# Adding up the value pairs of layer A's x and x1 on GpSimd before the product, and taking two tiles step by step together

## The chip, the cores and the metric

The kernel runs on one core of one Trainium2 chip. The metric is the device time of one execution in microseconds (us), lower is better. Before the change it is 2796.8 us, the median of three runs (2795.46 to 2797.88).

A core has five engines that run their own instruction queues in order and wait for one another by semaphores: TensorE (PE: matrix products and transposes; its weight loads are shown as PEld), VectorE (DVE), ScalarE (ACT), GpSimd (POOL) and SyncE (SP), which here issues nearly all transfers.

## The reference, cut to what matters

Sequence length 2048, width 1024, one layer A and one layer B, all in float32. The change touches layer A after its pooling mixer: the output projection with its residual (giving x1), and the gated embedding (giving x2).

```python
def reference(x, p, ...):
    for i in range(DEPTH):                      # DEPTH = 2
        if i < N_A:                             # layer A, i = 0
            h = rms_norm(x, a_norm[i])
            x = x + pool_mixer(h, a_w_in[i], a_w_group[i], a_scale[i], a_w_out[i])   # x1
        else:                                   # layer B: attention against shared K/V
            ...
            x = x + (o * jax.nn.silu(z)) @ b_w_out[j]
        x = x + (p[i] @ ple_w[i]) * jax.nn.sigmoid(x @ ple_gate_w[i])                # x2 for i = 0
    return x
```

## The kernel before

All activations of layer A are kept transposed: 8 tiles of 128 channels by 512 positions (index o = 0..7). The 2048 positions are worked in four chunks, s = 0..3. To keep float32 accuracy in products whose operands TensorE takes in a rounded form, each operand is stored as a **pair**: a tile [128, 2, 512] whose first half is the value rounded by a ScalarE copy, and whose second half is the rest, value minus rounded value (`split`, lines 213 to 215). A product takes three matmuls for each pair of operands (`product`, lines 131 to 133): high weight by high activation, high by low, low by high. The sum of the two halves of a pair is the value itself, up to float32 rounding.

Per chunk there are 22 steps, in this order: 4 times two steps for the z and u halves of the input projection (groups g = 3, 2, 1, 0; `run_z`, `run_u`, the latter with the pooling), 4 steps of the output projection (`run_o`, b = 0..3), 4 steps of the gate (`run_g`, b = 0..3), and 6 steps for q, k and v (`run_kvq`). After the last chunk comes the attention (layer B). Each step of `run_o` and `run_g` makes two output tiles, o = 2b and 2b + 1, each with 8 x 3 matmuls over the 8 input tiles, the two tiles interleaved; `run_g` adds 12 matmuls with the embedding p. Weights are loaded and split one step ahead (line 718): from HBM into `wraw`, ScalarE copies the high half (L106, or L112 with a gain), GpSimd or VectorE subtracts for the low half (L108, or L113 on VectorE). In the same steps, some weights of layer B are split and stored for later (`keep`: kraw, kpair).

The code is given to a scheduler that orders the instructions of each engine ahead of time; where the order matters to the author it is pinned (`keep_in_program_order`). At run time each engine takes its list in that order.

Around the change:

- `run_o` multiplies the mixer's output (tiles mp) by the output weights into PSUM (psd). The first two steps put off the last two input tiles.
- `residual` makes x1: VectorE adds PSUM and the high half of x's pair (L467), GpSimd adds the low half (L468), then ScalarE's copy (L214) and VectorE's subtraction (L215) make x1's pair, one tile after the other.
- `load_p` transposes the embedding p (L482) and splits it (ple).
- `run_g` multiplies all 8 x1 pairs by the gate weights, in the order o = 0..7, and ple by its weights; then, tile by tile, sigmoid on ScalarE (L498), multiply on VectorE (L499), add x1's low half on GpSimd (L500), add its high half on VectorE (L502), store the sum (L503), split it into x2's pair (L214, L215), store that (L507), square it (L510) and add the squares over the tiles (L513).
- `run_kvq` multiplies the 8 x2 pairs, again in the order 0..7, by the q, k and v weights (L525). After its first 48 matmuls, L534 sums the squares over the channels.
- `tmp` gives tiles of one rotating pool of 8 buffers, shared by the tiles ta, sg, tx, sq, po, zr and others.

So TensorE comes to the tiles x1[6], x1[7] 36 and 42 matmuls into the first gate product of a chunk, and to x2[6], x2[7] 36 and 42 matmuls into the first q product; these tiles are made by the step just before.

Of the kernel before, what the change touches and what calls it, by code (L numbers as in the profile page):

```python
# [10 lines left out]
AF = mybir.ActivationFunctionType  # L11
ALU = mybir.AluOpType
# [17 lines left out]
def f(ap):  # L30
    return ap.bitcast(F32)
# [3 lines left out]
def trunk_kernel(ctx, tc, x, p, a_norm, a_w_in, a_w_group, a_scale, a_w_out, kv_norm, w_kv,  # L35
                 k_norm, b_norm, b_w_in, b_q_norm, b_w_out, ple_w, ple_gate_w, out):
    nc = tc.nc
    V, A, G, T = nc.vector, nc.scalar, nc.gpsimd, nc.tensor
# [81 lines left out]
    def wst(units, kt, hl, c0, n=P):  # L120
        kk = units[0].shape[2]
        return units[kt // kk][:, hl, kt % kk, c0 : c0 + n]

    def product(pss_, units, acts, c0s, order=None, beside=(), begin=True, end=True):


        beside = iter(beside)
        order = order or range(len(acts))
        for kt in order:
            for ps, c0 in zip(pss_, c0s):  # L130
                T.matmul(ps, wst(units, kt, 0, c0), acts[kt][:, 0], start=(begin and kt == order[0]), stop=False)  # L131
                T.matmul(ps, wst(units, kt, 0, c0), acts[kt][:, 1], start=False, stop=False)  # L132
                T.matmul(ps, wst(units, kt, 1, c0), acts[kt][:, 0], start=False,  # L133
                         stop=(end and kt == order[-1]))
            next(beside, None)
        for _ in beside:
            pass
# [6 lines left out]
    def pair(nm):  # L144
        return act.tile([P, 2, W5], F32R, tag="act", name=nm)
# [33 lines left out]
    with ExitStack() as st:  # L179
# [7 lines left out]
        def dense():  # L187
            state["d"] += 1
            return (psd if state["d"] % 3 else psboth).tile([P, W5], F32, tag="psd", name="psd")

        def turned():
            return pst.tile([P, 4, P], F32, tag="pst", name="pst")

        def tmp(nm):
            return t2.tile([P, W5], F32, tag="tmp", name=nm, bufs=8)
# [17 lines left out]
        def split(pr, src, lo):  # L213
            A.copy(out=pr[:, 0], in_=src)  # L214
            lo.tensor_tensor(out=pr[:, 1], in0=src, in1=f(pr[:, 0]), op=ALU.subtract)  # L215
# [198 lines left out]
        def run_u(s, g, wu):  # L414
# [4 lines left out]
            for k in range(2):  # L419
# [24 lines left out]
                else:  # L444
                    split(pr, po, V)

        def run_o(s, b, wo):
            ck = chunk[s]
            pss2 = [dense(), dense()]
            if b < 2:  # L450
                product(pss2, wo, ck["m"], (0, P), [6, 7, 4, 5, 2, 3], end=False)
                if not b:
                    ck["o"] = pss2, wo
                    return
                for (pss2, wo), b in ((ck.pop("o"), 0), ((pss2, wo), 1)):
                    product(pss2, wo, ck["m"], (0, P), [0, 1], begin=False)
                    residual(s, b, pss2)
                return
            product(pss2, wo, ck["m"], (0, P))
            residual(s, b, pss2)  # L460

        def residual(s, b, pss2):
            ck = chunk[s]
            for k in range(2):
                xp = ck["x"][2 * b + k]
                t = tmp("ta")
                V.tensor_tensor(out=t, in0=pss2[k], in1=f(xp[:, 0]), op=ALU.add)  # L467
                G.tensor_tensor(out=t, in0=t, in1=f(xp[:, 1]), op=ALU.add)  # L468
                pr = pair("x1")
                split(pr, t, V)  # L470
                ck.setdefault("x1", []).append(pr)

        def load_p(s):
            pin = [io.tile([P, 2, PLE], F32, tag="io", name="pin") for _ in range(2)]
            for e in range(2):
                t0 = s * W5 + e * 2 * P
                nc.sync.dma_start(out=pin[e], in_=p[0, 0, t0 : t0 + 2 * P, :].rearrange("(j q) n -> q j n", q=P))
            col = []
            for k in range(2):
                pt = turned()  # L480
                for j in range(4):
                    T.transpose(pt[:, j, :], pin[j // 2][:, j % 2, k * P : (k + 1) * P], ident)  # L482
                pr = pair("ple")
                split(pr, pt.rearrange("q j t -> q (j t)"), V)
                col.append(pr)
            chunk[s]["p"] = col

        def run_g(s, b, wg, wl):
            ck = chunk[s]
            if b == 0:  # L490
                load_p(s)
            pss2, pls = [dense(), dense()], [dense(), dense()]
            product(pss2, wg, ck["x1"], (0, P))
            product(pls, wl, ck["p"], (0, P))
            for k in range(2):
                o = 2 * b + k
                sg = tmp("sg2")
                A.activation(out=sg, in_=pss2[k], func=AF.Sigmoid)  # L498
                V.tensor_tensor(out=sg, in0=pls[k], in1=sg, op=ALU.mult)  # L499
                G.tensor_tensor(out=sg, in0=sg, in1=f(ck["x1"][o][:, 1]), op=ALU.add)  # L500
                t = tmp("tx2")
                V.tensor_tensor(out=t, in0=sg, in1=f(ck["x1"][o][:, 0]), op=ALU.add)  # L502
                nc.sync.dma_start(out=x2d[s][o], in_=t)  # L503
                pr = pair("x2")
                split(pr, t, V)
                if s + 1 < NSUB:
                    nc.sync.dma_start(out=x2p[s][o], in_=f(pr))  # L507
                ck.setdefault("x2", []).append(pr)
                sq = tmp("sq")
                A.activation(out=sq, in_=t, func=AF.Square)  # L510
                if o:
                    na = t2.tile([P, W5], F32, tag="acc", name="acc")
                    G.tensor_tensor(out=na, in0=ck["acc"], in1=sq, op=ALU.add)  # L513
                    sq = na
                ck["acc"] = sq
# [152 lines left out]
        for s in range(NSUB):  # L668
            for g in (3, 2, 1, 0):
                def load(g=g, s=s, z=0):  # L670
                    if not s and z and g < 3:
                        chunk[0]["fold"][g] = load_fold(g)
                    if not s and not z:
                        return (None,)
                    return (load_w(wp, a_w_in[0], KT, z * D + g * 256, 256, g_a, "wi"),)
                steps.append((lambda load=load: load(z=1), lambda *w, s=s, g=g: run_z(s, g, *w)))
                steps.append((load, lambda *w, s=s, g=g: run_u(s, g, *w)))
            for b in range(4):
                steps.append((lambda b=b: (load_w(wp, a_w_out[0], KT, b * 256, 256),),
                              lambda *w, s=s, b=b: run_o(s, b, *w)))  # L680
            for b in range(4):
                steps.append((lambda b=b: (load_w(wp, ple_gate_w[0], KT, b * 256, 256),
                                           load_w(wp, ple_w[0], 2, b * 256, 256)),
                              lambda *w, s=s, b=b: run_g(s, b, *w)))
            for kind, wsrc, base, gain in (("q", b_w_in[0], 0, g_b), ("k", w_kv, 0, g_kv), ("v", w_kv, D, g_kv)):
                for b in range(2):
                    def load(wsrc=wsrc, base=base, b=b, gain=gain, s=s, kind=kind):
                        return (load_w(wp, wsrc, KT, base + b * W5, W5, gain),)
                    steps.append((load, lambda *w, s=s, kind=kind, b=b: run_kvq(s, kind, b, *w)))
# [27 lines left out]
        for i, (_, run) in enumerate(steps):  # L717
# [10 lines left out]
            step, s = i % STEPS, i // STEPS  # L728
# [320 lines left out]
```

## Time and profile before

| | before |
|---|---|
| median of three runs | 2796.8 us (2795.46 to 2797.88) |
| profiled execution, its own time | 2798.39 us |
| its span, first to last instruction | 2796.3 us |
| mean granted TensorE clock | 0.996 |

The profile is of one execution. Its page gives the busy time of each engine; other views group instructions by line, list waits (who waited for whom, in total, how often, and the longest), or show instructions in order of time. In such a timeline a row has the start in us, the duration in us, engine, line and operation, the tile written and the tiles read, the shapes, how many instructions were merged into the row, and in brackets the idle time of the engine just before it and what ended it. The view by windows gives for a stretch of time its length and the busy time (and count) of PE, PEld, DVE, ACT and POOL, then the granted clock, the share of the transfer engines and GB/s; asked for one engine alone, it gives that engine's column only.

### The profile page before, as it was taken

How to read it: one execution, taken by the hardware profiler on the slowest of the kernel's cores; microseconds unless marked ns; L12 is line 12 of the kernel's file. 1: busy time of each engine (PE TensorE's matmuls, PEld its weight loads, DVE VectorE, ACT ScalarE, POOL GpSimd, SP SyncE). 2: the span in 40 equal slices, each digit the busy share in tenths (PEclk: the TensorE clock that was granted, in tenths of full speed). 3: DMA queues.
4: the chain of work that ended last, by engine and by line, in shares of the span. 5: the costliest groups of instructions: out<-in, count | busy, mean ns of one | idle time of the engine just before them, and what ended most of it. 6: DMA issues, size and time to landing. Idle time of an engine off the chain costs nothing. (4 is left out here: it accounts for less than half of the span.)

```text
span 2796.3 us, 40450 instructions
## 1 busy us (share of the span) xinstructions
PE 2739.2 (98%) x13715; PEld 2265.2 (81%) x13715; DVE 1892.1 (68%) x2573; ACT 1388.3 (50%) x2801; POOL 928.9 (33%) x949
## 2 busy tenths in 40 slices
PE   9999999999999999999999999999999999999999
PEld 7878888878887888878878888887878778878877
DVE  6645634455354543545499999999999988885642
ACT  5434533355234552345356566566666665564431
POOL 2554336543475424753222112112211122213220
PEclk9999999999999999999999999999999999999999
DMA  8654696546955489444678565555555565658865
GB/s 284 239 173 160 231 315 230 181 166 220 339 194 192 157 258 315 151 145 151 196 252 276 181 222 169 170 163 185 162 162 163 183 184 183 200 181 250 256 202 161
DMA packets 335844, 573.28 MB, mean 205 GB/s; under 512 B 32463, under 2 KB 166639, under 8 KB 335637
## 3 DMA queue, kind: packets, MB, share of 16 engines
q1 hardware_dynamic: 330186, 563.03, 61.9%
q10 hardware_dynamic: 5450, 7.66, 0.9%
q8 instruction: 108, 1.77, 0.3%
q14 instruction: 100, 0.81, 0.1%
HBM read 430.01 MB, written 132.19 MB: 201 GB/s over the span
## 5 line engine op out<-in xcount | busy, mean ns | idle before, releaser
L525 PE MATMUL psd<-wpair,x 128*128 128x512 f32 x2304 | 548.4, 394 | 4.5 <-ACT x L214 3.6
L802 ACT CAST at<-psa 128x512 fp32r<-128x512 f32 (+3 forms) x640 | 333.0, 521 | 396.0 <-PE psa L799 390.3
L785 DVE TENSOR_TENSOR_SCAN pp<-kap,pp,zeros 128x512 f32<-128x512 f32 x384 | 508.0, 1324 | 5.5 <-ACT kap L778 3.9
L525 PEld LDWEIGHTS psd<-wpair,x 128*128 128x128 f32 x2304 | 429.5, 189 | 93.5 <-ACT x L214 5.0
L803 DVE TENSOR_TENSOR at<-psa,at 128x512 fp32r<-128x512 f32 (+3 forms) x640 | 379.7, 595 | 57.6 <-ACT at L802 54.9
L799 PE MATMUL psa<-ident,pp 128*128 128x128 f32 x2176 | 346.5, 275 | 21.7 <-DVE at L803 17.6
L778 ACT ACTIVATE kap<-psl 128x512 f32<-128x512 f32 (+3 forms) x640 | 343.7, 538 | 18.4 <-PE psl L775 15.1
L799 PEld LDWEIGHTS psa<-ident,pp 128*128 128x128 f32 x2176 | 263.4, 140 | 99.7 <-DVE at L803 42.2
L774 PE MATMUL psl<-kk,qa 128*128 128x512 f32 (+3 forms) x640 | 280.6, 438 | 0.7 <-ACT kap L778 0.7
L780 POOL TENSOR_SCALAR_AFFINE_SELECT kap<-kap 128x128 f32<-128x128 f32 x256 | 92.2, 361 | 558.1 <-ACT kap L778 534.7
L785 DVE TENSOR_TENSOR_SCAN pp<-kap,zeros 128x128 f32<-128x128 f32 (+3 forms) x256 | 215.9, 844 | 43.0 <-POOL kap L780 38.4
L811 PE MATMUL pso<-at,vv 128*128 128x512 f32 (+3 forms) x640 | 234.6, 367 | 1.3 <-ACT at L802 1.2
L812 PE MATMUL pso<-at,vv 128*128 128x512 f32 (+3 forms) x640 | 235.5, 368 | 0.0
L775 PE MATMUL psl<-kk,qb 128*128 128x512 f32 (+3 forms) x640 | 234.1, 366 | 0.0
L131 PE MATMUL psd<-xp,wpair 128*128 128x512 f32 x512 | 202.2, 396 | 1.7 <-ACT xp L268 1.2
L132 PE MATMUL psd<-xp,wpair 128*128 128x512 f32 x512 | 200.6, 392 | 0.0
L133 PE MATMUL psd<-xp,wpair 128*128 128x512 f32 x512 | 200.3, 391 | 0.0
L113 DVE SCALAR_TENSOR_TENSOR wpair<-wraw,gains,wpair 128x512 fp32r<-128x512 f32 x192 | 151.8, 811 | 31.2 <-ACT wpair L112 30.9
L108 POOL TENSOR_TENSOR wpair<-wraw,wpair 128x512 fp32r<-128x512 f32 x99 | 137.9, 1402 | 87.0 <-ACT wpair L106 66.8
L112 ACT ACTIVATE wpair<-wraw,gains 128x512 fp32r<-128x512 f32 x192 | 134.0, 717 | 35.4 <-PE psd L525 33.8
L811 PEld LDWEIGHTS pso<-at,vv 128*128 128x128 f32 x640 | 120.5, 188 | 28.0 <-ACT at L802 2.3
L812 PEld LDWEIGHTS pso<-at,vv 128*128 128x128 f32 x640 | 120.4, 188 | 24.7
(210 smaller groups left out, 5399.9 us busy)
## 6 DMA issues: line engine op xcount, KB each, us to landing
kk<-kd SPq DMA_DIRECT2D x320, 128.0 KB
vv<-vd SPq DMA_DIRECT2D x160, 256.0 KB
wraw<-in_w_kv_dram SPq DMA_DIRECT2D x128, 256.0 KB
wpair<-wzd SPq DMA_DIRECT2D x64, 512.0 KB
wpair<-wod SPq DMA_DIRECT2D x64, 512.0 KB
wpair<-wgd SPq DMA_DIRECT2D x64, 512.0 KB
wpair<-wu SPq DMA_DIRECT2D x48, 512.0 KB
wpair<-wi SPq DMA_DIRECT2D x36, 512.0 KB
```

The lines of the kernel that those rows point to most:

```text
L131: T.matmul(ps, wst(units, kt, 0, c0), acts[kt][:, 0], start=(begin and kt == order[0]), stop=False)
L132: T.matmul(ps, wst(units, kt, 0, c0), acts[kt][:, 1], start=False, stop=False)
L525: T.matmul(pss2[i], ck["x2"][kt][:, xh, tk], wst(ws, kt, wh, 0, W5), start=(kt == 0 and xh == 0 and wh == 0), stop=(kt == KT - 1 and wh == 1))
L774: T.matmul(ps[:, :w], qa[:, qs], kk[:, :w], start=True, stop=False)
L775: T.matmul(ps[:, :w], qb[:, qs], kk[:, :w], start=False, stop=True)
L778: A.activation(out=kp[:, r0:], in_=ps[:, :w], func=AF.Sigmoid, scale=-1.0)
L785: V.tensor_tensor_scan(out=pp[:, r0:][:, ::-1], data0=kp[:, r0:][:, ::-1], data1=zeros.to_broadcast([P, w]), initial=1.0 if st["diag"] els ...
L799: T.transpose(pt[:, j * P : (j + 1) * P], pp[:, r0 + kt * P : r0 + (kt + 1) * P], ident)
L802: A.copy(out=at[:, 0, cs], in_=pt[:, cs])
L803: V.tensor_tensor(out=at[:, 1, cs], in0=pt[:, cs], in1=f(at[:, 0, cs]), op=ALU.subtract)
L811: T.matmul(po[:, cs], vv[:, kt, :], at[:, 0, cs], start=(st["diag"] and kt == 0), stop=False)
L812: T.matmul(po[:, cs], vv[:, kt, :], at[:, 1, cs], start=False, stop=(st["last"] and kt == 3))
```

## The change

A helper `whole` adds the two halves of pairs on GpSimd into new `tmp` tiles. `run_o` and `run_g` call it at their start, ahead of the product; `residual` and `run_g` then make one VectorE add each with the whole value, where before a VectorE add of the high half and a GpSimd add of the low half were made. In both places the two tiles of a step are also taken together: both sums, then both splits; in `run_g` both sigmoids, then multiply and add for each, then stores and splits, then squares.

```diff
+        def whole(prs, nm):
+            ts = []
+            for pr in prs:
+                ts.append(tmp(nm))
+                G.tensor_tensor(out=ts[-1], in0=f(pr[:, 0]), in1=f(pr[:, 1]), op=ALU.add)
+            return ts
+
         def run_o(s, b, wo):
             ck = chunk[s]
+            ts = whole(ck["x"][2 * b : 2 * b + 2], "ta")
             pss2 = [dense(), dense()]
             if b < 2:
                 product(pss2, wo, ck["m"], (0, P), [6, 7, 4, 5, 2, 3], end=False)
                 if not b:
-                    ck["o"] = pss2, wo
+                    ck["o"] = pss2, wo, ts
                     return
-                for (pss2, wo), b in ((ck.pop("o"), 0), ((pss2, wo), 1)):
+                for (pss2, wo, ts), b in ((ck.pop("o"), 0), ((pss2, wo, ts), 1)):
                     product(pss2, wo, ck["m"], (0, P), [0, 1], begin=False)
-                    residual(s, b, pss2)
+                    residual(s, ts, pss2)
                 return
             product(pss2, wo, ck["m"], (0, P))
-            residual(s, b, pss2)
-
-        def residual(s, b, pss2):
+            residual(s, ts, pss2)
+
+        def residual(s, ts, pss2):
             ck = chunk[s]
-            for k in range(2):
-                xp = ck["x"][2 * b + k]
-                t = tmp("ta")
-                V.tensor_tensor(out=t, in0=pss2[k], in1=f(xp[:, 0]), op=ALU.add)
-                G.tensor_tensor(out=t, in0=t, in1=f(xp[:, 1]), op=ALU.add)
+            for t, ps in zip(ts, pss2):
+                V.tensor_tensor(out=t, in0=ps, in1=t, op=ALU.add)
+            for t in ts:
                 pr = pair("x1")
                 split(pr, t, V)
                 ck.setdefault("x1", []).append(pr)
...
             if b == 0:
                 load_p(s)
+            ts = whole(ck["x1"][2 * b : 2 * b + 2], "tx2")
             pss2, pls = [dense(), dense()], [dense(), dense()]
             product(pss2, wg, ck["x1"], (0, P))
             product(pls, wl, ck["p"], (0, P))
+            sgs = [tmp("sg2"), tmp("sg2")]
             for k in range(2):
-                o = 2 * b + k
-                sg = tmp("sg2")
-                A.activation(out=sg, in_=pss2[k], func=AF.Sigmoid)
-                V.tensor_tensor(out=sg, in0=pls[k], in1=sg, op=ALU.mult)
-                G.tensor_tensor(out=sg, in0=sg, in1=f(ck["x1"][o][:, 1]), op=ALU.add)
-                t = tmp("tx2")
-                V.tensor_tensor(out=t, in0=sg, in1=f(ck["x1"][o][:, 0]), op=ALU.add)
+                A.activation(out=sgs[k], in_=pss2[k], func=AF.Sigmoid)
+            for k in range(2):
+                V.tensor_tensor(out=sgs[k], in0=pls[k], in1=sgs[k], op=ALU.mult)
+                V.tensor_tensor(out=ts[k], in0=sgs[k], in1=ts[k], op=ALU.add)
+            for k in range(2):
+                o, t = 2 * b + k, ts[k]
                 nc.sync.dma_start(out=x2d[s][o], in_=t)
                 pr = pair("x2")
                 split(pr, t, V)
                 if s + 1 < NSUB:
                     nc.sync.dma_start(out=x2p[s][o], in_=f(pr))
                 ck.setdefault("x2", []).append(pr)
+            for k in range(2):
+                o, t = 2 * b + k, ts[k]
                 sq = tmp("sq")
                 A.activation(out=sq, in_=t, func=AF.Square)
```

In the changed code the add in `whole` is line 452, the add in `residual` line 474, the sigmoid 505, multiply and add 507 and 508.

## The prediction

> **What bounds the kernel now.** I read the page first, then TensorE's list of waits, then its timeline around those waits, then the granted clock there. The page has TensorE busy for all but 57.1 us of the span.
>
> ```profile
> PE 2739.2 (98%) x13715; PEld 2265.2 (81%) x13715; DVE 1892.1 (68%) x2573; ACT 1388.3 (50%) x2801; POOL 928.9 (33%) x949
> ```
>
> So a change to the other engines can only give back time in which TensorE stands still or runs slowly. Its list of waits holds four entries that the changed lines feed (columns: total us, times, longest):
>
> ```profile
> PE psd L131 <- ACT x L214: 4.7, 5, 3.3
> PE psd L525 <- ACT x L214: 3.6, 3, 2.2
> ...
> PE psd L132 <- DVE x L215: 1.6, 5, 0.6
> ...
> PE psd L525 <- DVE x L215: 0.9, 4, 0.2
> ```
>
> L131 and L132 wait for x1 (written by the residual of the output projection, read by the gate product), L525 waits for x2 (written by the gate step, read by the q product). Recorded idle time: 4.7 + 3.6 + 1.6 + 0.9 = 10.8 us. That is too small a price, because matmuls overlap and the record of one ends late. I therefore price each wait by start times. A clean spacing comes from 42 matmuls in 9.68 us (first row below): less the 0.39 of the last one, 9.29 / 41 = 0.227 us each, so 48 take 10.88.
>
> ```profile
> 180.32 0.48 PE L131 MATMUL psd<-x,wpair 128*128 128x512 f32 x1
> ...
> 192.03 0.79 PE L131 MATMUL psd<-x,wpair 128*128 128x512 f32 x1 [3.29 <-ACT x L214]
> ...
> 197.96 0.40 PE L131 MATMUL psd<-ple,wpair 128*128 128x512 f32 x1
> ...
> 517.94 0.48 PE L131 MATMUL psd<-x,wpair 128*128 128x512 f32 x1
> ...
> 530.26 0.39 PE L131 MATMUL psd<-ple,wpair 128*128 128x512 f32 x1
> ...
> 854.81 0.48 PE L131 MATMUL psd<-x,wpair 128*128 128x512 f32 x1
> ...
> 868.52 0.39 PE L131 MATMUL psd<-ple,wpair 128*128 128x512 f32 x1
> ...
> 1188.47 0.48 PE L131 MATMUL psd<-x,wpair 128*128 128x512 f32 x1
> ...
> 1201.03 0.39 PE L131 MATMUL psd<-ple,wpair 128*128 128x512 f32 x1
> ```
>
> ```profile
> 241.52 9.68 PE L525 MATMUL psd<-wpair,x 128*128 128x512 f32 x42
> ...
> 253.88 1.02 PE L534 MATMUL pst<-ones,acc 128*128 128x1 f32 x8
> 254.76 1.61 PE L525 MATMUL psd<-wpair,x 128*128 128x512 f32 x6
> ...
> 573.78 9.68 PE L525 MATMUL psd<-wpair,x 128*128 128x512 f32 x42
> ...
> 588.14 1.70 PE L534 MATMUL pst<-ones,acc 128*128 128x1 f32 x8
> 589.70 23.97 PE L525 MATMUL psd<-wpair,x 128*128 128x512 f32 x96
> 613.51 1.03 PE L627 MATMUL pst<-ident,qn 128*128 128x128 f32 x8
> ...
> 912.04 9.68 PE L525 MATMUL psd<-wpair,x 128*128 128x512 f32 x42
> ...
> 924.43 1.02 PE L534 MATMUL pst<-ones,acc 128*128 128x1 f32 x8
> ```
>
> The first gate product of each chunk is 48 matmuls from its first L131 to the first ple row. Loss above 10.88: chunk s=0 17.64 - 10.88 = 6.8; s=1 12.32 - 10.88 = 1.4; s=2 13.71 - 10.88 = 2.8; s=3 12.56 - 10.88 = 1.7. Together 12.7 us at x1, of which some 0.1 each is the first step after the transposes and stays: 12.3. The first q product, also 48, up to L534: s=0 12.36 - 10.88 = 1.5; s=1 14.36 - 10.88 = 3.5; s=2 12.39 - 10.88 = 1.5; s=3 I count as nothing. Behind the stall of s=1 the loss goes on: L534 takes 589.70 - 588.14 = 1.56 instead of 254.76 - 253.88 = 0.88 (0.7 more), and the next 96 matmuls 613.51 - 589.70 = 23.81 instead of 96 x 0.227 = 21.8 (2.0 more). Together 9.2 us at x2. Why a wait of 2 or 3 us costs more than itself is in the clock (last columns: granted clock, DMA share, GB/s):
>
> ```profile
> 192.00:198.00 6.00, 5.64 (x13) 4.03 (x14) 3.59 (x5) 3.14 (x6) 3.27 (x3) 0.51 0.52 179
> ...
> 586.00:594.00 8.00, 7.78 (x25) 6.35 (x25) 1.47 (x3) 2.77 (x6) 2.88 (x4) 0.57 0.22 89
> ```
>
> After the two longest stalls TensorE runs at half clock for about 6 us each.
>
> **The change, part by part.** Nothing is added or removed: per chunk, GpSimd has 8 adds for x1 and 8 for x2 before (L468, L500) and 8 and 8 after, VectorE and ScalarE the same counts, and no DMA is new. In the built program TensorE's order is unchanged; on the others the instructions move. So the arithmetic costs 0 in sum and all hangs on positions.
>
> *x1.* Before, from the product's end: VectorE add, GpSimd add, ScalarE cast, VectorE subtract. After, the GpSimd add has been made during the product and drops out of the chain. In s=0:
>
> ```profile
> 184.41 1.28 DVE L467 TENSOR_TENSOR ta<-psd,xp 128x512 f32<-128x512 f32 x2
> ...
> 186.84 0.62 ACT L214 CAST kpair<-kraw 128x512 fp32r<-128x512 f32 x1 [3.81 <-DMA kraw<-in_b_w_out_dram]
> 187.37 1.14 ACT L106 CAST wpair<-wraw 128x512 fp32r<-128x512 f32 x2
> ...
> 190.07 1.25 POOL L468 TENSOR_TENSOR ta<-ta,xp 128x512 f32<-128x512 f32 x1
> 191.36 0.62 ACT L214 CAST x<-ta 128x512 fp32r<-128x512 f32 x1 [2.85 <-POOL ta L468]
> 192.01 1.09 DVE L215 TENSOR_TENSOR x<-ta,x 128x512 fp32r<-128x512 f32 x1 [6.32 <-ACT x L214]
> ```
>
> The sum in psd was read by 185.69, but the GpSimd add came only at 190.07: it stood in GpSimd's queue behind weight work that waited for ScalarE and a kraw transfer. Without it ScalarE's queue is next in line: kpair cast, two L106 casts, done 188.51, then x1[6] at 189.13, its low part 0.69 to 1.09 later, x1[7] 0.62 behind. TensorE wants x1[6] after 36 matmuls, 180.32 + 8.2 = 188.5. If the kraw transfer lands no earlier, a stall of some 1.6 us stays (0.6 for the high part, the rest for the low one) and 5.2 of 6.8 come back; if it lands earlier, all. It should land earlier, since the loads' buffers are freed by weight subtractions that today stand behind L468; I take off 0.5 of the 1.6. In the other chunks the same sum ends in time; s=1, where VectorE reads psd latest:
>
> ```profile
> 521.74 1.28 DVE L467 TENSOR_TENSOR ta<-psd,xp 128x512 f32<-128x512 f32 x2
> ```
>
> Both sums stand at 523.0, two casts and two subtractions of 0.6 to 0.7 each bring the last low part to about 525.0, and x1[6] is wanted at 517.94 + 8.2 = 526.1.
>
> *x2.* Before, each of the two tiles goes through sigmoid, multiply, GpSimd add, VectorE add, cast, subtract, and the second tile's sigmoid stands behind the first tile's cast in ScalarE's queue. s=1, the worst:
>
> ```profile
> 577.56 0.68 DVE L499 TENSOR_TENSOR sg<-psd,sg 128x512 f32<-128x512 f32 x1
> ...
> 580.38 0.62 ACT L214 CAST x<-tx 128x512 fp32r<-128x512 f32 x1 [3.11 <-DVE tx L502]
> ...
> 581.43 0.58 ACT L498 ACTIVATE sg<-psd 128x512 f32<-128x512 f32 x1
> ...
> 582.93 1.27 POOL L500 TENSOR_TENSOR sg<-sg,x 128x512 f32<-128x512 f32 x1
> 584.23 0.69 DVE L502 TENSOR_TENSOR tx<-sg,x 128x512 f32<-128x512 f32 x1 [1.50 <-POOL sg L500]
> 584.96 0.62 ACT L214 CAST x<-tx 128x512 fp32r<-128x512 f32 x1 [2.95 <-DVE tx L502]
> ```
>
> The products are done at 573.9, the last cast ends at 585.6, 11.7 us later, while TensorE wants x2[7] 42 matmuls after 573.78, at 583.3. After: both sigmoids run while the ple product still runs; from 573.9 two multiplies (1.4), two adds (1.4), cast and square of the first tile (1.25), cast of the second (0.62), a weight subtraction of 0.74 and two of 0.69 on VectorE beside them: high parts by 578.6, low parts by about 579.5. x2[6] is wanted at 573.78 + 8.2 = 582.0. Spare: over 2 us. Even 577.56 as the first multiply, should VectorE's weight queue hold it as today, gives 577.56 + 2.8 + 1.9 = 582.2 for x2[7]'s high part, ahead of 583.3. So the 9.2 go. The waits next in TensorE's list are of the attention part and not touched.
>
> A rule of the Trainium skill (TensorE: Matmul & The Clock Gate, "What's actually happening") says that the clock halves after about one idle window of 3.4 us. In s=1 the list has only 2.2 us of idle before the half clock; by the rule that slow stretch need not be the wait's work, and the sum would be 2.7 less; I go by the rows, where both slow stretches begin right at the two longest waits.
>
> *Sum.* 12.3 - 0.5 + 9.2 = 21.0 us. The profiled execution took 2798.4 us (span 2796.3, 2.1 around it), 1.6 above the median of the three runs, 2796.8; a difference in the span carries over, so 2796.8 - 21.0 = 2775.8. I say 2776.
>
> **The rivals.**
>
> *Only one of the two places gains.* The early add of step b=3 stands, in the changed order, behind a square-sum add of step b=2 on GpSimd. For s=1: step 2 ends 60 matmuls (13.6 us) before 573.8, at 560.2; multiplies, adds, cast and square 4.1, the sum 1.3, gives 565.6, two early adds at the longest that a row shows (below) 3.5, gives 569.1, against a need at 575.3. It would have to be 6 us later. Against it speaks that margin. Price if x2 keeps its stalls: 2796.8 - 11.8 = 2785.0; if x1 keeps them: 2787.6.
>
> *Slower: a bunch of adds ahead of the weights.* Before the output projection, GpSimd's new order has five or six x1 adds in a row, the third and fifth waiting for buffers that VectorE frees late in the pooling step (L439); behind them stand the weight subtractions L108 and a kpair subtraction whose store holds SP's queue and every load behind it.
>
> ```profile
> L468 POOL TENSOR_TENSOR ta<-ta,xp x32: 1253/1506/1764, 158.5 to 1196.6; 128x512 f32<-128x512 f32 x32
> ```
>
> ```profile
> 473.00:518.00 45.00, 29.17 (x24) 1.00 0.48 148
> ```
>
> Eight adds at 1.76 are at most 14.1 us. Weights are loaded one step ahead, so their lead is at least a step of 48 matmuls, 10.9: up to 3.2 us late, the size of the wait that costs 6.8 in s=0. Once in each chunk that is 27 us: 2775.8 + 27 = 2803. It decides from 10.9 us of delay. Against it: GpSimd works only 29.2 of 45 us in this stage (second row), the adds are the same ones drawn forward, and TensorE's list has no wait for L108.
>
> *The half clock of s=1 has another cause* than the wait and stays: 2.7 less gain, 2778.5. For it, that the listed wait there is a third shorter than the one of s=0; against it, that the slow stretch follows it at once.
>
> *Nothing comes of it*: a queue of loads or casts holds x1 and x2 just as long as GpSimd does, 2796.8. For it, 186.84 above, where a transfer, not GpSimd, is late; against it, the 3 us between that and 190.07.
>
> **How the numbers follow.** Forecast with all or nearly all stalls gone: 0.66 (2772 to 2780). Half clock of s=1 stays: 0.06. One place only: 0.12. Nothing: 0.06. Slower: 0.10. Range: the low end is the full 22.1 with s=3's x2 and the 1.2 by which runs lie below or above their median, with some 1.5 for transfers that land earlier everywhere, 2772; the high end takes in the one-sided case, 2788; left out are some 0.18. A measurement of this kernel tells a change from none at about 0.2%, 5.6 us: faster 0.84, same 0.06, slower 0.10.
>
> **What would show it.** TensorE's list without L131/L132 waits for x and without L525 waits for x, or with under 1.5 us in all; 48 matmuls in about 10.9 us from the first gate row to the first ple row in every chunk and from the first L525 to L534; granted clock 1.0 in both places; the x1 adds (L452) well before their L474. Wrong would be: waits of TensorE for wpair in the output projection, a new wait for psd, or x2 casts that still end over 9 us after the ple product.

## The result, and the profile after

| | before | after |
|---|---|---|
| median | 2796.8 us (2795.46 to 2798.8, 5 runs) | 2778.67 us (2778.29 to 2781.82, 5 runs) |
| ratio after / before | | 0.9935, 95% interval [0.9922, 0.9949] |
| span of the profiled execution | 2796.3 us | 2779.0 us |
| first attention matmul in it | 1384.48 us | 1366.24 us |

The gain is 18.1 us; 21 were forecast. All of it was made before the attention: in the profiled executions its first matmul starts 18.24 us earlier, and 0.9 of that is lost again behind it, where nothing was changed.

The page of the changed kernel, its line of busy times:

```profile
PE 2729.7 (98%) x13715; PEld 2261.3 (81%) x13715; DVE 1950.7 (70%) x2573; ACT 1390.0 (50%) x2801; POOL 956.8 (34%) x949
```

The counts of instructions are those of before, and TensorE's order is too. But VectorE is busy 58.6 us longer (1950.7 against 1892.1) and GpSimd 27.9 us longer with the same instructions; that was not in the prediction and comes back below.

TensorE's list of waits after the change (total us, times, longest):

```profile
PE psa L809 <- DVE at L813: 17.7, 33, 1.4
...
PE psd L132 <- DVE x L215: 2.0, 2, 1.1
```

The two entries of L525 (L535 in the new numbering) are gone, and of the x1 waits two of about 1 us are left. The timeline of TensorE shows which; first the gate products, from the first gate row to the first ple row of each chunk, with the two waits between:

```profile
180.26 0.48 PE L131 MATMUL psd<-x,wpair 128*128 128x512 f32 x1
...
191.73 0.39 PE L131 MATMUL psd<-ple,wpair 128*128 128x512 f32 x1
...
510.15 0.48 PE L131 MATMUL psd<-x,wpair 128*128 128x512 f32 x1
...
521.14 0.39 PE L131 MATMUL psd<-ple,wpair 128*128 128x512 f32 x1
...
839.57 0.48 PE L131 MATMUL psd<-x,wpair 128*128 128x512 f32 x1
...
849.18 0.50 PE L132 MATMUL psd<-x,wpair 128*128 128x512 f32 x1 [0.95 <-DVE x L215]
...
852.13 0.39 PE L131 MATMUL psd<-ple,wpair 128*128 128x512 f32 x1
...
1170.52 0.48 PE L131 MATMUL psd<-x,wpair 128*128 128x512 f32 x1
...
1180.50 0.51 PE L132 MATMUL psd<-x,wpair 128*128 128x512 f32 x1 [1.09 <-DVE x L215]
...
1183.47 0.39 PE L131 MATMUL psd<-ple,wpair 128*128 128x512 f32 x1
```

Then the first q product of the first two chunks:

```profile
235.26 11.05 PE L535 MATMUL psd<-wpair,x 128*128 128x512 f32 x48
246.15 0.95 PE L544 MATMUL pst<-ones,acc 128*128 128x1 f32 x8
...
564.66 11.05 PE L535 MATMUL psd<-wpair,x 128*128 128x512 f32 x48
575.55 0.95 PE L544 MATMUL pst<-ones,acc 128*128 128x1 f32 x8
```

By the measure of the prediction (48 matmuls in 10.88 us) x1 now loses 11.47 - 10.88 = 0.6, then 0.1, 1.7 and 2.1 us, 4.5 in all against 12.7 before; x2 loses nothing, 10.89 in every chunk. The half clock is gone. The windows over the first gate product and over the q product of s=1 (length; busy time of PE, PEld, DVE, ACT, POOL; granted clock; share of the transfer engines; GB/s):

```profile
180.26:191.73 11.47, 11.43 (x51) 8.94 (x50) 7.82 (x10) 6.22 (x12) 7.40 (x6) 1.00 0.67 211
...
564.66:575.55 10.89, 10.89 (x49) 9.01 (x48) 5.08 (x7) 2.92 (x5) 3.33 (x2) 1.00 0.43 169
```

So x1 gave 12.7 - 4.5 = 8.2 instead of 11.8, and x2 the other 10.0 of the 18.24 instead of 9.2. The shortfall sits in the chunks s=2 and s=3. The timeline of s=2, all engines but TensorE, around the wait at 849.18:

```profile
840.49 1.30 POOL L108 TENSOR_TENSOR wpair<-wraw,wpair 128x512 fp32r<-128x512 f32 x1 [1.30 <-ACT wpair L106]
...
842.26 1.27 DVE L474 TENSOR_TENSOR ta<-psd,ta 128x512 f32<-128x512 f32 x2
845.34 0.62 ACT L214 CAST kpair<-kraw 128x512 fp32r<-128x512 f32 x1 [4.40 <-DMA kraw<-in_ple_gate_w_dram]
845.87 1.14 ACT L106 CAST wpair<-wraw 128x512 fp32r<-128x512 f32 x2
...
846.91 1.14 ACT L214 CAST x<-ta 128x512 fp32r<-128x512 f32 x2
...
847.56 3.26 DVE L215 TENSOR_TENSOR x<-ta,x 128x512 fp32r<-128x512 f32 x2 [4.02 <-ACT x L214]
```

and the transfer in it, in the timeline of SP:

```profile
841.82 0.37 SPq L702 DMA_DIRECT2D kraw<-in_ple_gate_w_dram  x1
```

Read it backwards. TensorE waits for the low part of x1[6] (L215). That waits for ScalarE's copy at 846.91. The sum it copies is complete at 843.53, but ahead of it in ScalarE's queue stands the copy kpair, and ScalarE sits idle for 4.40 us until the kraw transfer lands. That load was issued at 841.82, at once when GpSimd's weight subtraction ended (840.49 + 1.30 = 841.79) and let go of its buffer. So x1 is still held up over GpSimd, no longer by an add in x1's own chain but by weights that are late. The row 840.49 also says that GpSimd itself had stood idle for 1.30 us just then, waiting for ScalarE's copy of that weight: the lateness comes from further back in the chain, and the traces of e9 below show from where.

### The profile page after: what moved, and what is told of

It is laid out like the page before. It is cut to its first block, busy times and chain, and to the rows that moved or that the text cites. A ratio compares the mean times of both kernels' runs of the same rounds, so it can differ in the third digit from the quotient of the medians.

```text
span 2779.0 us, 40467 instructions
## 1 busy us (share of the span) xinstructions
PE 2729.7 (98%) x13715; PEld 2261.3 (81%) x13715; DVE 1950.7 (70%) x2573; ACT 1390.0 (50%) x2801; POOL 956.8 (34%) x949
## 5 line engine op out<-in xcount | busy, mean ns | idle before, releaser
L535 PE MATMUL psd<-wpair,x 128*128 128x512 f32 x2304 | 543.8, 393 | 0.0
L535 PEld LDWEIGHTS psd<-wpair,x 128*128 128x128 f32 x2304 | 428.1, 188 | 86.2
L113 DVE SCALAR_TENSOR_TENSOR wpair<-wraw,gains,wpair 128x512 fp32r<-128x512 f32 x192 | 170.6, 909 | 36.6 <-ACT wpair L112 33.2
L108 POOL TENSOR_TENSOR wpair<-wraw,wpair 128x512 fp32r<-128x512 f32 x99 | 144.4, 1475 | 60.4 <-ACT wpair L106 60.4
```

Of the source, the lines that this page charges most:

```text
L535: T.matmul(pss2[i], ck["x2"][kt][:, xh, tk], wst(ws, kt, wh, 0, W5), start=(kt == 0 and xh == 0 and wh == 0), stop=(kt == KT - 1 and wh == 1))
```

## The experiments

Losses are in us over the four chunks, counted as in the prediction; 0.4 of each x1 figure is the first step after the transposes. Runs of one group (e1 to e4, e5 to e7, e8 to e11) shared a chip and its runs of the kernel before, whose medians were 2798.23, 2799.62 and 2800.98 us; kernels of different groups are therefore compared by the ratio.

| kernel | median us (range) | ratio to before [95%] | loss at x1 | loss at x2 |
|---|---|---|---|---|
| before (first profile) | 2796.8 | 1 | 12.7 | 9.2 |
| after | 2778.67 (2778.29 to 2781.82) | 0.9935 [0.9922, 0.9949] | 4.5 | 0 |
| e1 x1 part alone | 2782.74 (2780.88 to 2783.94) | 0.9946 [0.9931, 0.996] | 0.7 | 8.9 |
| e2 x2 part alone | 2792.3 (2790.38 to 2795.06) | 0.9982 [0.9973, 0.9991] | 16.0 | 0 |
| e3 two-tile order in the gate step alone | 2790.96 (2787.54 to 2793.62) | 0.9969 [0.9959, 0.998] | 12.6 | 1.1 |
| e4 early add in the gate step alone | 2792.7 (2788.35 to 2796.98) | 0.9981 [0.9972, 0.999] | 15.2 | 0 |
| e5 all early adds on VectorE | 2774.52 (2772.97 to 2774.88) | 0.9911 [0.9898, 0.9925] | 0.4 | 0 |
| e5b early x2 adds on VectorE | 2776.07 (2775.03 to 2778.0) | 0.9919 [0.9905, 0.9932] | 1.9 | 0 |
| e6 kraw work moved | 2790.09 (2789.03 to 2791.68) | 0.9969 [0.9956, 0.9981] | 0.4 | 1.2 |
| e7 early x1 add, order alone at x2 | 2777.26 (2776.59 to 2779.29) | 0.9924 [0.9911, 0.9938] | 0.6 | 2.2 |
| e8 after, again | 2780.24 (2776.91 to 2781.96) | 0.993 [0.9917, 0.9942] | 5.0 | 0 |
| e9 early x1 adds on VectorE | 2775.52 (2774.81 to 2776.45) | 0.9914 [0.9901, 0.9928] | 0.4 | 0 |
| e10 before, its GpSimd adds on VectorE | 2776.32 (2773.85 to 2777.19) | 0.9915 [0.9902, 0.9929] | 0.4 | 0 |
| e11 as e5, again | 2775.49 (2773.74 to 2777.77) | 0.9914 [0.9901, 0.9928] | 0.4 | 0 |

The times follow the losses only roughly. e1 ran 15.5 us under the kernel before on its chip, where its losses are 12.3 us lower; and the first gate row, ahead of every loss counted here, lies between 176.8 us (e6) and 180.4 us (e9) in the profiles. What an edit does is therefore read from the losses.

**e1: the x1 part alone.** `run_o` and `residual` of after, `run_g` of before:

```diff
 def run_g(s, b, wg, wl):
-            ts = whole(ck["x1"][2 * b : 2 * b + 2], "tx2")
...
+                sg = tmp("sg2")
+                G.tensor_tensor(out=sg, in0=sg, in1=f(ck["x1"][o][:, 1]), op=ALU.add)
```

> Only the output projection's residual is changed, the gate step is as before. Theory (two separate gains, each by the TensorE stalls that it removes): the x1 losses fall as in the changed kernel, from 12.7 us above clean spacing to about 4.5, the x2 losses (10 us with the half clock behind them in s=1) stay; time 8.2 us below before, about 2788.6. Rival (the two places share one cause, a GpSimd queue that is late as a whole, so relieving one relieves the other): x2 losses fall too, gain over 12 us.

x1 loses only 0.7 us, less than in the whole change. The time fell by 15.5 us, more than the 8.2 expected and as far as the rival had it, but not for the rival's reason: x2 keeps its losses; they fall on other chunks than before (6.9 in s=0, 1.9 in s=2). TensorE's list:

```profile
PE psd L532 <- ACT x L214: 3.5, 2, 2.4
```

So the x1 part does all that was hoped for when it stands alone, and something in the x2 part takes 3.8 us of it back.

**e2: the x2 part alone.** `run_g` of after, `run_o` and `residual` of before.

```diff
+            ts = whole(ck["x1"][2 * b : 2 * b + 2], "tx2")
...
                 t = tmp("ta")
                 V.tensor_tensor(out=t, in0=pss2[k], in1=f(xp[:, 0]), op=ALU.add)
                 G.tensor_tensor(out=t, in0=t, in1=f(xp[:, 1]), op=ALU.add)
```

> Only the gate step is changed, the residual is as before. Theory: x2 losses go to nothing and the half clock after 586 us goes with them, x1 losses stay at about 12.7; gain 10 us, about 2786.8. Rival (one shared cause): x1 losses fall as well. Rival (the half clock of s=1 is not the wait's work): the granted clock still drops in s=1 around the first q product although its wait is gone; gain 7 us.

x2 is clear, but x1 loses 16.0, 3.3 more than before, so that 5.9 us are gained instead of the expected 10. The timeline of s=0 shows how:

```profile
187.55 1.25 POOL L108 TENSOR_TENSOR wpair<-wraw,wpair 128x512 fp32r<-128x512 f32 x1
188.77 1.25 POOL L493 TENSOR_TENSOR tx<-x 128x512 f32<-128x512 f32 x1
189.99 2.48 POOL L468 TENSOR_TENSOR ta<-ta,xp 128x512 f32<-128x512 f32 x2
191.27 0.62 ACT L214 CAST x<-ta 128x512 fp32r<-128x512 f32 x1 [4.06 <-POOL ta L468]
```

The first early x2 add (L493), whose result is first read at 205.99, 16 us after it is ready, runs on GpSimd just ahead of the add that x1[6] waits for (L468).

**e3 and e4: the gate step's two halves.** e3 has only the two-tile order, with GpSimd's add left behind the multiply; e4 has only the early add, tile by tile.

```diff
 e3
-            ts = whole(ck["x1"][2 * b : 2 * b + 2], "tx2")
...
+                G.tensor_tensor(out=sgs[k], in0=sgs[k], in1=f(x1[:, 1]), op=ALU.add)
+                V.tensor_tensor(out=ts[k], in0=sgs[k], in1=f(x1[:, 0]), op=ALU.add)
 e4
-                G.tensor_tensor(out=sg, in0=sg, in1=f(ck["x1"][o][:, 1]), op=ALU.add)
-                t = tmp("tx2")
-                V.tensor_tensor(out=t, in0=sg, in1=f(ck["x1"][o][:, 0]), op=ALU.add)
+                t = ts[k]
+                V.tensor_tensor(out=t, in0=sg, in1=t, op=ALU.add)
```

> Before, with only the order of the gate step changed: both sigmoids, then multiply and both adds for each tile (GpSimd low half, VectorE high half, behind the multiply as before), then stores and splits, then squares. No early add. Theory A (the early add is what removes the x2 stall): GpSimd's adds stay in the chain, 2.6 us for two tiles; much of the x2 loss stays, gain under 4 us. Theory B (the order is what removes it, because the second tile's sigmoid and multiply no longer stand behind the first tile's cast): chain from the end of the ple product 0.7 + 1.3 + 1.3 + 0.7 + 0.6 = 4.6 us and some waits, still ahead of the 9.5 us that TensorE gives; x2 losses go, gain 9 to 10 us, about 2787.

> Before, with only the early add in the gate step: one GpSimd add of the pair's halves ahead of the product, then tile by tile as before (sigmoid, multiply, one add, store, split, square). Theory A (the early add is what counts): x2 losses go, gain 9 to 10 us. Theory B (the order is what counts): the second tile still waits for the first tile's cast and square in ScalarE's queue; one GpSimd add of 1.3 us with its waits, some 2 us, drops out per tile, 4 us for both, against a loss of 3.5 in s=1 and 1.5 in s=0 and s=2. Both could be enough alone; then e3 and e4 both gain 9 to 10 us.

Either half clears x2 (1.1 and 0 left of 9.2); they don't add up. Only the early add raises the loss at x1, to 15.2; the order leaves it at 12.6. The gains are 7.3 and 5.5 us, where 9 to 10 were hoped for. This gave theory Q: the early x2 adds stand in GpSimd's queue ahead of weight subtractions, whose buffers the kraw load waits for.

**e5b and e5: early adds on VectorE**, in e5b those for x2, in e5 all.

```diff
-        def whole(prs, nm):
+        def whole(prs, nm, eng=G):
...
-                G.tensor_tensor(out=ts[-1], in0=f(pr[:, 0]), in1=f(pr[:, 1]), op=ALU.add)
+                eng.tensor_tensor(out=ts[-1], in0=f(pr[:, 0]), in1=f(pr[:, 1]), op=ALU.add)
...
+            ts = whole(ck["x1"][2 * b : 2 * b + 2], "tx2", V)
```

> The changed kernel with the early adds for x2 on VectorE instead of GpSimd; those for x1 stay on GpSimd. The changed kernel keeps losses at x1 of 0.6, 0.1, 1.7 and 2.1 us. Theory Q (the early x2 adds stand in GpSimd's queue ahead of weight subtractions, whose buffers the kraw load waits for, and with it ScalarE's copy of x1): the x1 losses fall to 0.7 us in all as in the run with the x1 part alone, x2 keeps none, 2.5 to 4 us less than the changed kernel, about 2775. Rival C (what stays at x1 comes from the early x1 adds, or from the load itself): the losses of the third and fourth chunk stay at 1.7 and 2.1 and the time is the changed kernel's, 2778.7. Second rival: VectorE, 70% busy, takes 8 more adds in each chunk and is late itself: new waits of TensorE for wpair or x, slower than the changed kernel.

> The changed kernel with all early adds, those for x1 and for x2, on VectorE. By theory Q the x1 losses go as in the run with only the x2 adds there, 2775. For the price of two engines side by side: where no GpSimd add of two SBUF operands runs, VectorE's subtraction of the low half (L215) has a longest time well under the 1.8 us of the changed kernel only if the adds were what slowed it; if the weight subtractions on GpSimd slow it as much, its longest time stays at 1.7 to 1.8 and its total changes little. Rival: 16 more adds per chunk on VectorE (11 us in each) delay the pooling or the weights: over 2779, with waits of TensorE for m or wpair.

e5b: the losses of s=2 and s=3 fall from 1.7 and 2.1 to 0.9 and 0.1. e5: none is left. The rival that VectorE comes late itself did not appear: no new wait of TensorE for wpair or m in either. For the price of two engines side by side, see the last section.

**e6: the kraw work moved** into the q, k, v steps of the first three chunks. The pieces of work are the same, only their places differ.

```diff
-            if step >= 8 and (s + 1 < NSUB or step < 16):
-                kept.pop(0)()
-                if s + 1 < NSUB and step in (8, 12):
+            if s + 1 < NSUB and step >= 16:
+                for _ in range(3 + (step == 16 and s < 2)):
                     kept.pop(0)()
```

> The changed kernel with all the preparation of layer B's weights (kraw, kpair) taken out of the steps of the output projection and the gate and put into the six q, k, v steps of the same chunks. Theory K (the copy of x1 waits in ScalarE's queue behind the copy kpair, and that for a late kraw transfer): the losses at x1 in the third and fourth chunk (1.7 and 2.1 us) fall under 0.5 each, and 3 to 4 us are gained, 2775, unless the q, k, v steps now lose some. Rival D (VectorE's subtraction for x1 is slowed by GpSimd beside it, 1.56 instead of 0.69 us): 0.9 us stays in each of these chunks, 2777. A gain of nothing at x1 would clear kraw altogether.

x1 loses nothing any more (11.0 us in every chunk), with all early adds still on GpSimd. That is what theory K expects, by which the copy of x1 was late because kpair stood before it. But the move also takes the kpair subtractions (1.3 us each) off GpSimd and the kraw loads out of these steps, so it shows that the kraw work as a whole is needed for the loss, and not the copy by itself. As a kernel it is no use, since the q, k, v steps cannot take the work: TensorE's list now has

```profile
PE pst L637 <- DVE xp L269: 11.6, 9, 2.8
```

**e7: early x1 add, and at x2 the order alone.** `run_o` of after, `run_g` of e3.

> The early add for x1 as in the changed kernel, and in the gate step only the two-tile order, with GpSimd's add of x1's low half left behind the multiply. Measured alone, the early x1 add left 0.7 us at x1 and the order left 1.1 us at x2. Theory Q: both together leave 1.8 us, against 4.5 at x1 and none at x2 in the changed kernel: 2.7 us less than that, 2776. Rival C (the rest at x1 does not come from the early x2 adds): x1 keeps some 3.9 us and x2 1.1, 2779.5.

x1 keeps 0.6, as theory Q has it; x2 keeps 2.2, in s=0, instead of 1.1. The time is 2777.26, between the two expectations, and decides nothing, since the changed kernel ran on other chips.

**e8, e9 and e11**, with e10 on one chip: the changed kernel again; early x1 adds on VectorE, x2's on GpSimd; e5 again.

```diff
 e9
-            ts = whole(ck["x"][2 * b : 2 * b + 2], "ta")
+            ts = whole(ck["x"][2 * b : 2 * b + 2], "ta", V)
```

> The changed kernel unchanged, once more, so that it shares its chip and its runs of the kernel before with the next three. Both theories: 2776 to 2782, 18 us under the kernel before, losses at x1 of some 4 to 5 us mainly in the third and fourth chunk. If those losses are small here, they are chance and not the order.

> The changed kernel with the early adds for x1 on VectorE and those for x2 left on GpSimd, the fourth of the four ways to place the two sets. Both on GpSimd kept 4.5 us at x1, x2's alone on VectorE kept 1.5, both on VectorE kept none. Theory Q (the x2 adds ahead of the weight subtractions are the cause): 3 us or more stay in the third and fourth chunk, time within 1.5 us of the changed kernel. Rival B (any eight adds less in GpSimd's queue will do, since it is the sum of its work that makes it late): the losses fall under 1.5 us, 3 us faster than the changed kernel.

> The changed kernel with all early adds on VectorE, once more beside the changed kernel itself: 3 to 6 us under it, no loss at x1 above 0.2 us in a chunk and none at x2. Rival: the difference seen in the run before was between chips, and the two are within 2 us.

The losses of the changed kernel come again (1.5, 0.1, 1.7 and 1.7), so they belong to its order. e9 goes against theory Q and for rival B: the early x2 adds are still on GpSimd, and the losses are gone. The same chain as above in s=2 of e9, SP's timeline first, then ScalarE and GpSimd:

```profile
836.15 0.37 SPq L702 DMA_DIRECT2D kraw<-in_ple_gate_w_dram  x1
```

```profile
834.83 1.29 POOL L108 TENSOR_TENSOR wpair<-wraw,wpair 128x512 fp32r<-128x512 f32 x1 [1.29 <-ACT wpair L106]
```

```profile
839.25 0.62 ACT L214 CAST kpair<-kraw 128x512 fp32r<-128x512 f32 x1 [3.99 <-DMA kraw<-in_ple_gate_w_dram]
839.78 1.14 ACT L106 CAST wpair<-wraw 128x512 fp32r<-128x512 f32 x2
...
840.82 1.14 ACT L214 CAST x<-ta 128x512 fp32r<-128x512 f32 x2
```

Again the load leaves when the weight subtraction ends (836.12), but against the first gate row (839.19 here) everything is over 5 us earlier. Where these 5 us arise is in GpSimd's timeline ahead of the output projection of the same chunk, first of the changed kernel, then of e9:

```profile
801.38 9.86 POOL L452 TENSOR_TENSOR ta<-xp 128x512 f32<-128x512 f32 x6
```

```profile
803.80 5.10 POOL L108 TENSOR_TENSOR wpair<-wraw,wpair 128x512 fp32r<-128x512 f32 x3 [1.20 <-ACT wpair L106]
```

In the changed kernel six early x1 adds run in a row, and the next weight subtraction starts only at 812.70; in e9 three of them follow each other from 803.80 on. The next kraw load is issued at 816.52 in the one and at 810.53 in the other, and from there the kpair and x1 copies on ScalarE come 5.5 to 6.1 us later in the changed kernel than in e9, up to the x1[6] of s=2. Two early x2 adds (2.95 us from 826.44 on) then stand ahead of the next weight subtractions; e9 has them too (2.93 us from 820.77 on). Without the x2 adds (e5b) 1.9 us of the 4.5 stay, without the x1 adds (e9) 0.4, which is the first step. So eight adds fewer in GpSimd's queue before the gate product help in either place, and those for x1 weigh more.

**e10: the kernel before, with its GpSimd adds on VectorE.** Nothing early, tile by tile:

```diff
-                G.tensor_tensor(out=t, in0=t, in1=f(xp[:, 1]), op=ALU.add)
+                V.tensor_tensor(out=t, in0=t, in1=f(xp[:, 1]), op=ALU.add)
...
-                G.tensor_tensor(out=sg, in0=sg, in1=f(ck["x1"][o][:, 1]), op=ALU.add)
+                V.tensor_tensor(out=sg, in0=sg, in1=f(ck["x1"][o][:, 1]), op=ALU.add)
```

> The kernel before with its 16 late GpSimd adds per chunk (L468, L500) on VectorE at the same place in the text: no early add, tile by tile. Theory Q1 (the x1 loss is the add standing in GpSimd's queue behind weight work): each add takes 0.7 us right behind the one before it, so x1 loses under 2 us in all; at x2 the tile by tile order stays, but without the hop to GpSimd, 1 to 3 us; 2781 to 2785, most of the gain without any early add. Rival T (it must be early, because ScalarE's queue is what comes next): x1 keeps 5 us or more, some 2789. Second rival: VectorE's weight subtractions come late by the added work, waits of TensorE for wpair.

It does better than theory Q1 hoped: no loss at x1, none at x2, 2776.32 us. The timeline of s=2 (its first gate row is at 838.92):

```profile
835.97 0.62 ACT L214 CAST kpair<-kraw 128x512 fp32r<-128x512 f32 x1 [2.46 <-DMA kraw<-in_ple_gate_w_dram]
...
837.64 1.38 DVE L467 TENSOR_TENSOR ta<-psd,xp 128x512 f32<-128x512 f32 x2 [3.41 <-PE psd L133]
...
838.93 2.53 DVE L468 TENSOR_TENSOR ta<-ta,xp 128x512 f32<-128x512 f32 x2
839.79 0.62 ACT L214 CAST x<-ta 128x512 fp32r<-128x512 f32 x1 [0.84 <-DVE ta L468]
```

kpair is copied 3 us before the gate product begins, and x1[6] follows its sum with 0.84 us of waiting. At x2 the chain is still tile by tile, but each hop costs 0.7 us on VectorE, and it is in time. So neither drawing the adds forward nor the two-tile order was needed: taking them off GpSimd is enough, and e10 and e11 can't be told apart (2773.85 to 2777.19 and 2773.74 to 2777.77). Both lie 4 to 5 us below the changed kernel on the same chip (2780.24, 2776.91 to 2781.96); that is about as much as a measurement can tell, but the traces show the same amount at x1.

The five kernels side by side in s=2, in us from the first gate row, from their timelines:

| | kraw load issued | kpair copy starts | x1[6] copy starts | x1[6] low part ends | loss |
|---|---|---|---|---|---|
| before | 0.9 | 3.5 | 8.1 | 9.9 | 2.8 |
| after | 2.2 | 5.8 | 7.3 | 9.6 | 1.7 |
| e1 | -0.1 | 3.8 | 5.4 | 7.6 | 0.1 |
| e9 | -3.0 | 0.1 | 1.6 | 3.8 | 0.1 |
| e10 | -5.7 | -3.0 | 0.9 | 3.1 | 0.1 |

In the kernels with the early x1 add, a chunk loses about what its x1[6] low part ends behind 7.9 us, a bound fitted to three chunks of the changed kernel: 9.55 gives 1.7 here, 9.92 gives 2.1 in s=3, 8.45 gives 0.6 in s=0.

## Why the prediction was right, and where it was not

- *What bounds.* Right. TensorE's order did not change, and the time moved by what its waits for x1 and x2 cost; the pricing by start times instead of recorded idle time held: 10.8 us of listed idle time could not have given 18. The total is nearer to the forecast than its parts: x1 gave 3.6 less than expected, x2 0.8 more.
- *x2, 9.2 us expected.* Right, 10.0: the 0.6 in s=3 that was counted as nothing came too, and the eight L534 after each q product take 0.81 instead of 0.88. The chain in s=1 was predicted with high parts 4.8 and low parts 5.7 us after the start of the q product; they end 3.2 and 5.1 after it. What the prediction had not seen is that either half of the gate change would have done it (e3, e4).
- *x1, 11.8 us expected.* Mechanism right, size wrong: 8.2. The step that failed is "In the other chunks the same sum ends in time". That sum began at VectorE's add and had the copies follow at once; the kpair copy that waits for kraw was reckoned with in s=0 only. There the prediction held (0.5 more than the clean 0.1 was allowed for, and 0.6 in all was lost), and in s=1 too. In s=2 and s=3 the same copy stood ahead of x1[6] and came 5.77 and 6.15 us after the first gate row. The argument that the load "should land earlier, since the loads' buffers are freed by weight subtractions that today stand behind L468" is true of s=0, where the copy came at 4.66 instead of 6.52 us, and wrong for s=2 and s=3, where it came later than before (5.77 instead of 3.54, 6.15 instead of 2.44): there the subtractions stand behind early adds. What the early adds cost the work behind them on GpSimd was put at nothing in the sum and weighed only as a rival. Moving the kraw work (e6) or eight adds (e9) takes the loss away, so that neither the kraw work nor the adds alone make it; that the copy in ScalarE's queue is the link between them is read from the trace of s=2 and not separated by a run. One of the signs that the prediction named was missed with it: the waits for x1 are 2.0 us in all, not under 1.5.
- *The second half of that miss* is the low part itself: taken at 0.69 to 1.09 us, it took 1.56 in s=2 (below). Of the 1.7 us lost there, 1.56 - 0.69 = 0.9 is that, the other 0.8 the late copy; this split is worked out, not measured by itself.
- *The half clock.* Right to go by the rows. The slow stretches went with their waits, as the two windows at clock 1.00 show. By the rule from the Trainium skill (TensorE: Matmul & The Clock Gate, "What's actually happening"), taken as a need for some 3.4 us of idle time in one wait, the sum would have been 18.3, by chance nearer to the measured 18.1; but the 2.7 us that it would have left in s=1 were not left.
- *The rivals.* One place only: no, both gained. Slower by a bunch of adds: no wait for wpair appeared in the output projection, but its mechanism (adds ahead of weights, loads behind them) is what kept 4 us, through the kraw load and at a smaller size: the six adds in a row took 9.86 us in s=2, less than the 10.9 from which it was to decide. Nothing, because a load holds x1 as long as GpSimd does: true for s=3, where x1 lost 1.7 before and 2.1 after.
- *Behind the first attention matmul* the profiled executions lose 0.9 us, which the medians do not show. The stretch from there to the end is 1411.8 us before, 1412.8 in after and 1411.5 in the same kernel's other profile (e8, 2778.2 - 1366.7), so that is variation between executions.

## What to carry to other kernels

When an operation leaves a chain, look at what stands next in each queue of that chain, in every chunk and not only in the worst one: here a copy of something else, waiting for a load, whose buffer the same busy engine had yet to free. Drawing work forward on a crowded in-order queue moves its cost to whatever stands behind it; ask first whether the work can leave that engine, which here was an edit of two words (e10) that gave no less than the whole rewrite, and by the losses 4 us more. And before building two remedies for one wait, price each alone: at x2 either would have done.

## What was not expected of the hardware

**VectorE and GpSimd slow each other.** The groups of the tile tx, x2's sum, after the change (count, then ns at least, median, most), and of its last row the same before:

```profile
L452 POOL TENSOR_TENSOR tx<-x x32: 1288/1740/1839, 166.8 to 1219.6; 128x512 f32<-128x512 f32 x32
...
L215 DVE TENSOR_TENSOR x<-tx,x x32: 677/1778/1799, 204.1 to 1230.3; 128x512 fp32r<-128x512 f32 x32
```

```profile
L215 DVE TENSOR_TENSOR x<-tx,x x32: 691/693/695, 208.5 to 1254.0; 128x512 fp32r<-128x512 f32 x32
```

The same subtraction takes 0.69 us alone and 1.78 beside a GpSimd operation, which itself goes from 1.29 to 1.74. Where VectorE reads PSUM, nothing of it: the 32 adds L474 of the tile ta lie within 13 ns, and one ran fully beside a GpSimd subtraction (second pair below).

```profile
L474 DVE TENSOR_TENSOR ta<-psd,ta x32: 671/676/684, 164.2 to 1173.7; 128x512 f32<-128x512 f32 x32
```

Single pairs, from two short stretches of the timeline around 847 and 838 us:

```profile
847.29 1.28 POOL L108 TENSOR_TENSOR wpair<-wraw,wpair 128x512 fp32r<-128x512 f32 x1
847.56 1.56 DVE L215 TENSOR_TENSOR x<-ta,x 128x512 fp32r<-128x512 f32 x1 [4.02 <-ACT x L214]
```

```profile
836.67 1.37 DVE L108 TENSOR_TENSOR wpair<-wraw,wpair 128x512 fp32r<-128x512 f32 x1 [5.04 <-ACT wpair L106]
...
837.46 1.74 POOL L108 TENSOR_TENSOR wpair<-wraw,wpair 128x512 fp32r<-128x512 f32 x1
837.97 0.68 DVE L474 TENSOR_TENSOR ta<-psd,ta 128x512 f32<-128x512 f32 x1
```

In the first pair VectorE ends 0.55 us after GpSimd (849.12 and 848.57), as if it had begun only then. In the second, GpSimd's 1.74 is not the work of the PSUM add: it started while VectorE's weight subtraction still ran, until 838.04, and ended 1.16 us behind that. The Trainium skill (SBUF — State Buffer, "SBUF: two separate sides") calls this an exclusive lock: a VectorE operation with two SBUF inputs and a GpSimd operation that reads SBUF share a pair of ports, and the later one blocks until the earlier has ended. The rows agree with that, and not with a sharing of bandwidth, which would have stretched GpSimd's 1.28 too. This is also where VectorE's 58.6 us lie: six of its groups with two inputs in SBUF grow by 61.8 us together with the same counts (L113 from 151.8 to 170.6, L215 of tx from 22.2 to 39.3), while the adds of the tile ta that read PSUM take 20.6 us before and 20.4 after. The early adds are not the only partner: in e5, without any of them on GpSimd, the median of L215 for x1 falls from 730 to 684 ns, but single ones still take 1.78 us beside the weight subtractions. The groups of the tile ta, after and then e5:

```profile
L215 DVE TENSOR_TENSOR x<-ta,x x32: 674/730/1782, 166.0 to 1180.4; 128x512 fp32r<-128x512 f32 x32
```

```profile
L215 DVE TENSOR_TENSOR x<-ta,x x32: 679/684/1782, 157.6 to 1171.1; 128x512 fp32r<-128x512 f32 x32
```

**Half clock after less than 3 us.** Behind three waits of TensorE the granted clock reads as follows: first the row with the wait, then the window behind it, in e6, in e9 and in e8.

```profile
345.65 0.66 PE L637 MATMUL pst<-ident,qn 128*128 128x128 f32 x4 [2.80 <-DVE xp L269]
...
346.00:350.00 4.00, 4.00 (x16) 3.20 (x15) 1.29 (x3) 1.57 (x3) 0.00 (x0) 0.57 0.95 328
```

```profile
111.92 0.66 PE L358 MATMUL pst<-ident,uraw 128*128 128x128 f32 x4 [1.97 <-DVE wt L215]
...
114.00:116.00 2.00, 2.00 (x10) 1.90 (x9) 0.00 (x0) 0.29 (x1) 2.00 (x2) 0.50 0.00 0
```

```profile
113.25 0.66 PE L358 MATMUL pst<-ident,uraw 128*128 128x128 f32 x4 [2.10 <-DVE wt L215]
...
115.00:117.00 2.00, 2.00 (x16) 1.89 (x15) 0.31 (x1) 0.87 (x3) 1.81 (x2) 1.00 0.00 0
```

Recorded waits of 2.2 us (before, s=1), 2.4 (e1), 2.8 (e6) and 1.97 (e9) were followed by half clock; waits of 2.10 (e8, and again e10), 1.8 and 1.7 (both e6) were not. The waits in e9 and e8 are at the same place of the program, and the shorter one was followed by half clock. So around 2 us the length of a wait alone does not decide it; what else does, no run here shows.
